# Two-layer streaming encoder on one core: an operand made a second time with the norm in it, a convolution that reads PSUM, and operand sums moved to the end of a stage

## The chip, the core and the metric

The kernel runs on one core of a Trainium2 chip. The metric is device time in microseconds (us), from the first instruction to the last. The engines in the text are PE (TensorE, matrix products), DVE (VectorE), ACT (ScalarE), POOL (GpSimd) and SP (SyncE, which here only starts transfers). ACT and POOL start transfers too, from their own instruction streams.

## The reference, cut to what matters

Two layers (`DEPTH = 2`), 512 positions, width 1024, everything in fp32:

```
h  = rmsnorm(x, norm1_g[i]);  z = h @ w_in[i] + b_in[i]
mq, mk = silu(causal_conv(z[..., :2048], conv_w[i], conv_b[i]))     # 4 taps along time
y_m = sigmoid(mo) * head_layernorm(mlstm(mq, mk, mv, mi, mf))       # 4 heads, 256 wide
y_r = silu(rg) * head_layernorm(retention(rope(rq), rope(rk), rv))  # 4 heads, 256 / 512 wide
x = x + (sigmoid(gm) * (y_m @ w_bm[i]) + sigmoid(gr) * (y_r @ w_br[i])) @ w_out[i]
x = x + relu(rmsnorm(x) @ w_ff1[i] + b_ff1[i])^2 @ w_ff2[i] + b_ff2[i]
x = x + sigmoid(rmsnorm(x) @ w_pe_gate[i]) * (p[i] @ w_pe[i])
```

The norm of a position is one number, `rstd(t)`. It can be multiplied into the operand `x * g` ahead of a product with `w_in`, or into the product's result behind it.

## The kernel before

**Products.** Activations lie transposed, as eight tiles of 128 features x 512 positions. Every fp32 operand is held as a high part (rounded to the fast fp32r form) and a low part (the rest), and a product is three matmuls (`mm3`: high x high, high x low, low x high). Weights come as a list of *units*. A `T8` unit gives one output tile 128x512 with 24 matmuls, each 512 wide. Four `V` units give the values of one head or of two (24 matmuls of 512 each). A `PAIR` unit gives two output tiles by a Strassen-Winograd scheme: seven products P1 to P7 of 12 matmuls, each 256 wide, in place of 48 matmuls that are 512 wide. It needs sums of the operand's quarters (`xs_sums`, four of them in a layer, each for two of the eight tiles of `x`) and sums of the weights' quarters, which POOL makes by software transfers, paced by the unit number. P1, P2 and P4 use the operand itself; P3, P5, P6 and P7 use its sums. P5 and P3 collect in one bank of PSUM, P1, P6 and P7 in another; after each product ACT or DVE takes out what stands there, before the next may write.

**Weights.** SP loads a unit's weights into one of four slots `wr`. ACT writes the high part `wh` (line 258), DVE the low part `wl` (line 259), two units ahead of the use.

**Order.** The code is written in the order of the stages. A scheduler of the framework then sets each engine's instruction order when the kernel is built; on the chip an engine works through its list in that order. A transfer that ACT starts is an instruction of ACT's list: if what it waits for is late, everything behind it in the list waits as well. Small working tiles come from a ring of six slots (`tmp`), PSUM has eight banks.

**A layer's first half.** `xa` is the operand `x * g` without the norm; `n1.b` is `rstd` spread over 128 rows, `n1.c` the same as columns. The stages are: the input and forget gates (`if`); the four query and key tiles of mLSTM head 0 (`l0m00` to `l0m03`, through the convolution); the values of heads 0 and 1 (`mv_vals(0)`); two tiles of the branch gate (`bgm0`, `bgm1`); then per head `m_scores`, `m_qk` of the next head (four `T8` and the convolution), `m_attend` (whose result `num` is scaled by DVE in `head_scale`, line 613), `m_out` (two output-gate tiles `o0`, `o1`, then PE transposes `num` into tiles `ot`, line 619). `xs_sums` follows `m_out(0)`, `m_out(1)`, `m_scores(2)` and `m_out(2)`, one each. Then come the retention's queries and keys (`r0brq`, `r0brk`), the product with `w_bm` (tiles `bm0` to `bm7`, each multiplied by a branch gate that is read back from `gm_spill` for the first four), and the retention heads.

**The convolution before** (`conv_evac`): DVE multiplies the PSUM tile by the norm into a padded tile `z` in SBUF (line 762), POOL fills three columns ahead of it, ACT makes the tap for the current position (line 765), DVE adds three shifted taps (line 767), ACT applies SiLU.

**Products of a PAIR before**: the norm is multiplied in behind them by `scaled` (two DVE operations 128x512 for each PAIR with `w_in`), the second with the sign that the scheme leaves.

Of the kernel before, what the change touches and what calls it, by code (L numbers as in the profile page):

```python
# [39 lines left out]
P = 128  # L41
# [15 lines left out]
PAD = 32  # L57
LAST = 4

# [42 lines left out]
def groups():  # L102

    g = {}
    for i in range(L):
# [7 lines left out]
        g[i, "gm"] = [("w_in", 0, CGM + 256 * p) for p in range(4)]  # L113
# [9 lines left out]
def unit_list(i):  # L123
# [39 lines left out]
    mo(0)  # L163
    mqk(2)
    v(CV + 512)
    mo(1)
    mqk(3)
    mo(2)
    pair("gm", 1)
    mo(3)  # L170
    rqk(0)
    for p in range(4):
        if p > 1:
            pair("gm", p)
        full("w_bm", 0, 0, 2 * p, 2 * p + 2)
    v(CRV)
# [32 lines left out]
def build(ctx, tc, ins, out):  # L209
# [50 lines left out]


    index = {g: k for k, g in enumerate(groups())}
    sums = {(g, x): tc.dram_tile([4, P, Q], F32, name=f"s{k}{x}") for g, k in index.items() for x in MADE}

    def block(g, x):
        return ins["wpairs"][index[g], GIVEN.index(x)] if x in GIVEN else sums[g, x]
# [265 lines left out]
    def rows_split_v(i, h, nm, n_, j, o, rc, bvt, vh, vl):  # L532

        t = tmp(f"{nm}v{j}")
        ve.scalar_tensor_tensor(t[:, :T], o, rc[:, j:j + 1], bvt, OP.mult, OP.add)
# [13 lines left out]
    def values(i, nm, act, nrm, bv_ap, n_):  # L549
# [3 lines left out]
        for u in range(4):  # L553
            _, wh, wl = unit("V")
            if u == 1:
                flush()
            for kk in range(2):
# [9 lines left out]
        for j in range(NT):  # L567
            rows_split_v(i, None, nm, n_, j, o[j], nrm.c, bvt, vh[j], vl[j])
# [53 lines left out]
    def gated(nm, o, nrm, func, bias):  # L622
        g = tmp(f"{nm}g")
        ve.tensor_tensor(g[:, :T], o, nrm.b, OP.mult)
        ac.activation(g[:, :T], g[:, :T], func, bias=bias)
        return g
# [92 lines left out]
    for i in range(L):  # L719
# [25 lines left out]


# [9 lines left out]
        def conv_tile(nm, c, qh, ql, q):  # L756
            conv_evac(t8(xa, f"{nm}z"), nm, c, qh, ql, q)

        def conv_evac(o, nm, c, qh, ql, q):
            z = cur["low"].tile([P, 576], F32, name=f"{nm}zp", tag="z", bufs=2)  # L760
            gp.tensor_copy(z[:, 0:3], negb[:, c:c + 1].to_broadcast([P, 3]))
            ve.tensor_tensor(z[:, 3:515], o, n1.b, OP.mult)
            a = tmp(f"{nm}cv")
            cw = [bc[:, i, ow + 16 * j + c:ow + 16 * j + c + 1] for j in range(4)]
            ac.activation(a[:, :T], z[:, 3:515], AF.Identity, bias=cbp[:, c:c + 1], scale=cw[3])
            for j in (2, 1, 0):
                ve.scalar_tensor_tensor(a[:, :T], z[:, j:j + T], cw[j], a[:, :T], OP.mult, OP.add)
# [12 lines left out]
        def m_qk(h):  # L780
            nm = f"l{i}m{h}"
            qk = qk_tiles(nm)
            for d in range(2):
                conv_tile(f"{nm}q{d}", 2 * h + d, qk[0][d], qk[1][d], True)
            for d in range(2):
                conv_tile(f"{nm}k{d}", 8 + 2 * h + d, qk[2][d], qk[3][d], False)
            return qk
# [24 lines left out]
        def m_attend(h, pt, vv):  # L812
# [3 lines left out]
            attend(nm, pt, vv[0], vv[1], (h % 2) * 258, 258, num)  # L816
            mv = head_stats(nm, num, 256)
            den = cols.tile([P, NT], F32, name=f"{nm}den", tag="den")
            dn = num[:, :, 256]
            ve.tensor_scalar(den, dn, -1.0, None, OP.mult)  # L820
            ve.tensor_tensor(den, den, dn, OP.max)
            ve.tensor_tensor(den, den, gem[:, :, h], OP.max)
            ve.reciprocal(den, den)
            hv = cols.tile([P, NT], F32, name=f"{nm}hv", tag="hv")
            ve.tensor_tensor(hv, mv[:, :, 1], den, OP.mult)
            ve.tensor_tensor(hv, hv, den, OP.mult)
            ve.tensor_scalar(hv, hv, EPS, None, OP.add)
            gp.tensor_tensor(hv, hv, nhalf, OP.pow)
            ve.tensor_tensor(hv, hv, den, OP.mult)
# [3 lines left out]
        def m_out(h, num):  # L833
            nm = f"l{i}m{h}o"
            gs = [gated(f"{nm}{v}", t8(xa, f"{nm}{v}"), n1, AF.Sigmoid, bcol(i, "bo", 2 * h + v)) for v in range(2)]
            gate_out(nm, gs, num, [bcol(i, "gmn", 2 * h + v) for v in range(2)], ym, 2 * h)

        def r_qk(h):
# [3 lines left out]
            def rope(a, bn):  # L842
                b = [bcol(i, bn, 2 * h + d) for d in range(2)]

                def consume(y):
                    for d in range(2):
                        scaled(d, y[d], n1, y[d])
                    for d in range(2):
                        u = tmp(f"{nm}{bn}u{d}")
                        w = tmp(f"{nm}{bn}w{d}")  # L850
                        ve.scalar_tensor_tensor(u, y[0], b[0], trig[d][:, :T], OP.add, OP.mult)
                        ve.scalar_tensor_tensor(w, y[1], b[1], trig[1 - d][:, :T], OP.add, OP.mult)
                        ve.tensor_tensor(u, u, w, (OP.subtract, OP.add)[d])
# [13 lines left out]
        def r_attend(h, pt, vv):  # L867
# [5 lines left out]
            ve.tensor_scalar(hv, mv[:, :, 1], EPS, None, OP.add)  # L873
# [4 lines left out]
        def r_out(h, num, y):  # L878
# [3 lines left out]
            def gates(w):  # L882
                def consume(g):
                    for d in range(2):
                        scaled(d, g[d], n1, g[d])
                        ac.activation(g[d], g[d], AF.Silu, bias=bcol(i, "brg", 4 * h + 2 * w + d))
                        gs[2 * w + d] = g[d]
# [12 lines left out]
        def gm_gates(p):  # L900

            def consume(g):
                for d in range(2):
                    scaled(d, g[d], n1, g[d])
                    gm_done(2 * p + d, g[d])
# [3 lines left out]
        def gm_done(c, g):  # L909
            ac.activation(g, g, AF.Sigmoid, bias=bcol(i, "bgm", c))  # L910
            if c < 4:
# [463 lines left out]
```

## Time and profile before

| what | value |
|---|---|
| median of three runs | 2421.15 us (2416.18 to 2422.08) |
| the profiled execution | 2422.81 us; its span 2421.1 us |
| PE busy | 2365.9 us, 98% of the span, 13860 matmuls |
| DVE busy | 1646.8 us, 68% |
| ACT busy | 1203.1 us, 50% |
| POOL busy | 257.9 us, 11% |
| mean granted PE clock | 0.989 |

The span is the time between the first and the last recorded instruction; the 1.7 us between it and the execution's time lie around it. A busy share is an average over the stages. PE's clock is the share of its full rate that the chip granted. "Waits" lists for how long an engine sat idle until a named instruction of another engine was done.

### The profile page before, as it was taken

Reading aid. Unit: us, or ns where it says so; the run is one execution under the profiler, and the core shown is the slowest. Engines: PE = TensorE matmul, PEld = TensorE weight load, DVE = VectorE, ACT = ScalarE, POOL = GpSimd, SP = SyncE. Lnnn points to the kernel's source line nnn. Section 1 sums busy time; section 2 is a strip of 40 time slices with the busy share of each in tenths; the row PEclk is TensorE's granted clock in tenths of the full one; section 3 lists DMA queues with packets and bytes.
Section 4 is the critical chain, followed back from the end, with each engine's and each line's share of the span. In section 5 each row is a group of like instructions: output and inputs, shape, how many; then the busy total and the mean of one; then the engine's idle time right before and its main releaser. Section 6 shows DMA issues by size and latency. Waiting matters only on the chain.

```text
span 2421.1 us, 35877 instructions
## 1 busy us (share of the span) xinstructions
PE 2365.9 (98%) x13860; PEld 2094.6 (87%) x13860; DVE 1646.8 (68%) x2553; ACT 1203.1 (50%) x1745; POOL 257.9 (11%) x366
## 2 busy tenths in 40 slices
PE   9898999999999999999999979999999999999997
PEld 8787888998998898899887868899989988998996
DVE  7777747775676576667777677477837756676675
ACT  5656534553454445445557554344525545455463
POOL 3211000000001200001311110000000020000011
PEclk9999999999999999999999989999999999999998
DMA  7877686667788877778766658866686885443441
GB/s 240 216 202 196 197 264 185 198 185 240 194 256 261 231 235 206 221 242 221 233 178 191 183 161 240 239 177 205 186 240 192 282 248 158 153 141 120 144 154 44
DMA packets 183371, 487.68 MB, mean 201 GB/s; under 512 B 17936, under 2 KB 20368, under 8 KB 183200
## 3 DMA queue, kind: packets, MB, share of 16 engines
q1 hardware_dynamic: 119952, 281.82, 34.9%
q0 software_dynamic: 43520, 167.78, 29.4%
q10 hardware_dynamic: 19728, 35.79, 4.2%
q8 instruction: 108, 1.77, 0.3%
q14 instruction: 63, 0.52, 0.1%
HBM read 470.64 MB, written 182.45 MB: 270 GB/s over the span
## 4 chain that ended last, share of the span: by engine, by line
PE 44%; DVE 3%; ACT 1%; issue 1%; DMA 1%; POOL 0%; POOLq 0%; DVEq 0%; ACTq 0%
PE l1f L345 2%; PE l1f L346 2%; PE l1f L347 2%; PE l1br L347 1%; PE l1br L345 1%; PE l1br L346 1%; PE l1wo L345 1%; PE l1bm L347 1%; PE l1wo L347 1%; PE l1wo L346 1%; PE l1bm L345 1%; PE l1bm L346 1%; DMA wr<-s11t 0%; DVE wl L259 0%; PE l1pg L345 0%
## 5 line engine op out<-in xcount | busy, mean ns | idle before, releaser
L258 ACT ACTIVATE wh<-wr 128x1024 fp32r<-128x1024 f32 x250 | 264.1, 1058 | 394.3 <-issue 61.8
L259 DVE TENSOR_TENSOR wl<-wr,wh 128x1024 fp32r<-128x1024 f32 x250 | 307.1, 1229 | 159.0 <-ACT wh L258 158.4
L258 ACT ACTIVATE wh_C<-wr 128x1024 fp32r<-128x1024 f32 x78 | 82.5, 1058 | 131.2 <-DMA wr<-wstream 8.8
L259 DVE TENSOR_TENSOR wl_B<-wr,wh_B 128x1024 fp32r<-128x1024 f32 x78 | 95.4, 1223 | 45.4 <-ACT wh_B L258 45.3
L258 ACT ACTIVATE wh_B<-wr 128x1024 fp32r<-128x1024 f32 x78 | 82.3, 1055 | 75.4 <-PE l0r1vp L563 3.6
L258 ACT ACTIVATE wh_A<-wr 128x1024 fp32r<-128x1024 f32 x78 | 82.4, 1057 | 71.6 <-PE l1f L346 11.3
L259 DVE TENSOR_TENSOR wl_A<-wr,wh_A 128x1024 fp32r<-128x1024 f32 x78 | 96.6, 1238 | 23.6 <-ACT wh_A L258 23.6
L258 ACT ACTIVATE wh_D<-wr 128x512 fp32r<-128x512 f32 x78 | 49.1, 629 | 123.5 <-DMA wr<-s11t 10.4
L259 DVE TENSOR_TENSOR wl_C<-wr,wh_C 128x1024 fp32r<-128x1024 f32 x78 | 95.2, 1221 | 22.1 <-ACT wh_C L258 21.3
L259 DVE TENSOR_TENSOR wl_D<-wr,wh_D 128x512 fp32r<-128x512 f32 x78 | 53.6, 688 | 80.7 <-ACT wh_D L258 73.8
L345 PE MATMUL l1f<-l1n2h,wh 128*128 128x512 f32 x256 | 99.8, 390 | 0.0
L345 PE MATMUL l0f<-l0n2h,wh 128*128 128x512 f32 x256 | 99.8, 390 | 0.0
L347 PE MATMUL l0f<-l0n2h,wl 128*128 128x512 f32 x256 | 99.7, 389 | 0.0
L347 PE MATMUL l1f<-l1n2h,wl 128*128 128x512 f32 x256 | 99.7, 389 | 0.0
L346 PE MATMUL l0f<-l0n2l,wh 128*128 128x512 f32 x256 | 99.6, 389 | 0.0
L346 PE MATMUL l1f<-l1n2l,wh 128*128 128x512 f32 x256 | 99.6, 389 | 0.0
L347 PEld LDWEIGHTS l0f<-l0n2h,wl 128*128 128x128 f32 x256 | 48.1, 188 | 10.2
L347 PEld LDWEIGHTS l1f<-l1n2h,wl 128*128 128x128 f32 x256 | 48.1, 188 | 10.2
L346 PEld LDWEIGHTS l0f<-l0n2l,wh 128*128 128x128 f32 x256 | 48.1, 188 | 9.8
L345 PEld LDWEIGHTS l1f<-l1n2h,wh 128*128 128x128 f32 x256 | 48.1, 188 | 9.8
L346 PEld LDWEIGHTS l1f<-l1n2l,wh 128*128 128x128 f32 x256 | 48.1, 188 | 9.7
L345 PEld LDWEIGHTS l0f<-l0n2h,wh 128*128 128x128 f32 x256 | 48.1, 188 | 9.6
(5788 smaller groups left out, 8368.0 us busy)
## 6 DMA issues: line engine op xcount, KB each, us to landing
wr<-wstream SPq DMA_DIRECT2D x250, 512.0 KB, 4.5
wr<-wpairs SPq DMA_DIRECT2D x234, 256.0 KB, 3.7
s0t<-wpairs POOLq DMA_DIRECT2D x6, 1024.0 KB, 9.1
s1t<-wpairs POOLq DMA_DIRECT2D x6, 1024.0 KB, 9.3
s2t<-wpairs POOLq DMA_DIRECT2D x6, 1024.0 KB, 8.8
s3t<-wpairs POOLq DMA_DIRECT2D x6, 1024.0 KB, 10.0
s4t<-wpairs POOLq DMA_DIRECT2D x6, 1024.0 KB, 9.3
s5t<-wpairs POOLq DMA_DIRECT2D x6, 1024.0 KB, 8.5
```

What stands on the lines that cost most here:

```text
L258: ac.activation(hi_ap, src, AF.Copy)
L259: ve.tensor_sub(lo_ap, src, hi_ap.bitcast(F32))
L345: te.matmul(o, sh, mh, start=first, stop=False)
L346: te.matmul(o, sh, ml, start=False, stop=False)
L347: cur["mm"] = te.matmul(o, sl, mh, start=False, stop=last)
```

## The change

1. A second operand `xn = x * g * rstd` is made in each layer, in eight steps `xn_tile(k)`: ACT starts a transfer of `x` tile k into a `tmp` slot, DVE multiplies (128x512), ACT writes the high part, DVE the low part. Tiles 0 to 3 are made beside `bgm0` and `bgm1`, tiles 4 to 7 beside the four tiles of `m_qk(1)`. Everything of the layer from the output gates of head 0 on uses it: the output gates, `m_qk(2)` and `m_qk(3)`, the second values group, `bgm2` and `bgm3`, all retention products and all PAIRs. There no norm is multiplied in behind the product: `scaled` is gone, and gates and taps read PSUM directly. `xa` is released after `m_qk(1)`, and the tiles of the operand sums take its place.
2. The convolution works on the PSUM tile: for heads 0 and 1 DVE multiplies it by the norm in place, ACT and DVE read the taps from PSUM, and a 128x3 addition (`fix`) mends the first three positions. The padded tile and POOL's copy are gone. The bank is held until the last tap.
3. The first four gate tiles are all `T8` units (before: two `T8` and a PAIR).
4. `xs_sums(0)` to `xs_sums(3)` stand together, after the values of retention head 0 and ahead of `bm0` to `bm3` and `r_qk(0)`. DVE applies gain and norm there (before: ACT the gain).
5. One unit more stands ahead of the transposes: in heads 0 and 2 the tiles `bgm2` and `bgm3`, in head 1 two units of the values, in head 3 the output gates ahead of `m_attend` and two units of the values of retention head 0 (`rv_vals(0)`, moved ahead of `bm`).
6. A few small column operations of the head norm go to POOL, and the chain of the denominator is shorter.

The built orders count 168 matmuls of 256 columns fewer and 96 of 512 more, 102 DVE instructions fewer, 16 more transfers of 256 KB on ACT.

```diff
-        g[i, "gm"] = [("w_in", 0, CGM + 256 * p) for p in range(4)]
+        g[i, "gm"] = [("w_in", 0, CGM + 256 * p) for p in (2, 3)]
...
-    def scaled(d, y, nrm, out_):
-        if d:
-            ve.scalar_tensor_tensor(out_, y, -1.0, nrm.b, OP.mult, OP.mult)
-        else:
-            ve.tensor_tensor(out_, y, nrm.b, OP.mult)
...
+        def conv_evac(o, nm, c, qh, ql, q, nrm):
             a = tmp(f"{nm}cv")
             cw = [bc[:, i, ow + 16 * j + c:ow + 16 * j + c + 1] for j in range(4)]
-            ac.activation(a[:, :T], z[:, 3:515], AF.Identity, bias=cbp[:, c:c + 1], scale=cw[3])
+            if nrm:
+                ve.tensor_tensor(o, o, nrm.b, OP.mult)
+            ac.activation(a[:, :T], o, AF.Identity, bias=cbp[:, c:c + 1], scale=cw[3])
             for j in (2, 1, 0):
-                ve.scalar_tensor_tensor(a[:, :T], z[:, j:j + T], cw[j], a[:, :T], OP.mult, OP.add)
+                t = slice(3 - j, T)
+                ve.scalar_tensor_tensor(a[:, t], o[:, :T - 3 + j], cw[j], a[:, t], OP.mult, OP.add)
+            ve.tensor_tensor(a[:, 0:3], a[:, 0:3], fix[:, :, c], OP.add)
...
+        def normed(nm, k):
+            t = tmp(f"l{i}{nm}{k}")
+            nc.scalar.dma_start(t, x_src[k])
+            ve.scalar_tensor_tensor(t, t, n1.col(k), n1.b, OP.mult, OP.mult)
+            return t
+
+        def xn_tile(k):
+            split(normed("xnr", k), xn[0][k], xn[1][k])
...
         def xs_sums(k):
-            t = [tmp(f"l{i}xsr{k}{a}") for a in range(2)]
-            for a in range(2):
-                nc.scalar.dma_start(t[a], x_src[2 * k + a])
-                ac.activation(t[a], t[a], AF.Copy, scale=n1.col(2 * k + a))
+            t = [normed("xsr", 2 * k + a) for a in range(2)]
...
         num = m_attend(0, pt, vv)
-        m_out(0, num)
-        xs_sums(0)
+        gs = m_gates(0)
+        gm_tile(2, xn, None)
+        m_back(0, gs, num)
...
         pt = m_scores(3, qk)
-        gm_gates(1)
+        gs = m_gates(3)
         num = m_attend(3, pt, vv)
-        m_out(3, num)
+        vv = rv_vals(0, lambda: m_back(3, gs, num))
...
+        for k in range(4):
+            xs_sums(k)
...
+        for c in range(4):
+            bm_tile(c)
         qk = r_qk(0)
```

**Three places of the order.** On DVE, at the start of the first layer, `cv` tiles are the convolution's sums, `ql` a low part that it leaves, and `wl_0_663` is the low weights of `bgm0`. Before:

```order
L767 SCALAR_TENSOR_TENSOR l0m00cv<-l0m00zp,bc,l0m00cv 128x512
L767 SCALAR_TENSOR_TENSOR l0m01cv<-l0m01zp,bc,l0m01cv 128x512
L762 TENSOR_TENSOR l0m02zp<-l0m0z_431,l0n1rb 128x512
L259 TENSOR_TENSOR wl_0_663<-wr_550,wh_0_662 128x1024
L762 TENSOR_TENSOR l0m03zp<-l0m0z_556,l0n1rb 128x512
L771 SCALAR_TENSOR_TENSOR l0m0ql_346<-l0m00cv,l0m0qh_345 128x512
```

After, where the low weights of `bgm0` are `wl_0_667`:

```order
L781 SCALAR_TENSOR_TENSOR l0m02cv<-l0m0z_439,bc,l0m02cv 128x511
L781 SCALAR_TENSOR_TENSOR l0m03cv<-l0m0z_561,bc,l0m03cv 128x511
L781 SCALAR_TENSOR_TENSOR l0m02cv<-l0m0z_439,bc,l0m02cv 128x510
L781 SCALAR_TENSOR_TENSOR l0m03cv<-l0m0z_561,bc,l0m03cv 128x510
L786 SCALAR_TENSOR_TENSOR l0m0ql_354<-l0m00cv,l0m0qh_353 128x512
L786 SCALAR_TENSOR_TENSOR l0m0ql_356<-l0m01cv,l0m0qh_355 128x512
L781 SCALAR_TENSOR_TENSOR l0m02cv<-l0m0z_439,bc,l0m02cv 128x509
L782 TENSOR_TENSOR l0m02cv<-l0m02cv,l0fix 128x3
L781 SCALAR_TENSOR_TENSOR l0m03cv<-l0m0z_561,bc,l0m03cv 128x509
L782 TENSOR_TENSOR l0m03cv<-l0m03cv,l0fix 128x3
L263 TENSOR_TENSOR wl_0_667<-wr_555,wh_0_666 128x1024
```

The weights of `bgm0` stood after the convolution of two tiles and now stand after that of four.

On ACT, beside attend and output gates of head 0 (after): `l0xnr_1134` is the load for the last tile of `xn`, `l0m1z_1099` the PSUM tile of head 1's last convolution, `l0m0a` the attend results.

```order
L608 ACTIVATE l0m0num<-l0m0a_1166 128x258
L608 ACTIVATE l0m0num<-l0m0a_1174 128x258
L608 ACTIVATE l0m0num<-l0m0a_1185 128x258
L262 ACTIVATE l0xnh<-l0xnr_1087 128x512
L783 ACTIVATE l0m12cv<-l0m12cv 128x512
L262 ACTIVATE wh_0_1224<-wr_999 128x1024
L262 ACTIVATE l0m1kh_948<-l0m12cv 128x512
L778 ACTIVATE l0m13cv<-l0m1z_1099,l0cbp,bc 128x512
L935 DMA l0xnr_1134<-xT 128x512
L783 ACTIVATE l0m13cv<-l0m13cv 128x512
L262 ACTIVATE l0m1kh_950<-l0m13cv 128x512
L262 ACTIVATE l0xnh<-l0xnr_1134 128x512
```

The load for the last tile stands behind the attend copies of head 0 and the last convolution of head 1; before, there was no such load.

On ACT, at the operand sums: `xsr` are the loads of `x`, `xsu` the sums, `xsh` their high parts. Before, `xs_sums(1)` stood within head 1:

```order
L936 DMA l0xsr_1832<-xT 128x512
L625 ACTIVATE l0m1o1g<-l0m1o1g,bc 128x512
L258 ACTIVATE l0ymh_333<-l0m1o0g 128x512
L936 DMA l0xsr_1833<-xT 128x512
L258 ACTIVATE l0ymh_335<-l0m1o1g 128x512
L937 ACTIVATE l0xsr_1832<-l0xsr_1832,bc 128x512
```

After, behind the values of retention head 0, the first two sets and the last:

```order
L935 DMA l0xsr_2690<-xT 128x512
L262 ACTIVATE wh_0_2793<-wr_2581 128x1024
L262 ACTIVATE l0xsh_1143<-l0xsu_2693 128x512
L935 DMA l0xsr_2703<-xT 128x512
L935 DMA l0xsr_2706<-xT 128x512
L262 ACTIVATE l0xsh_1145<-l0xsu_2694 128x512
```

```order
L262 ACTIVATE l0xsh_1155<-l0xsu_2741 128x512
L1034 DMA l0gml_2751<-gm_spill 128x512
L1034 DMA l0gml_2787<-gm_spill 128x512
L262 ACTIVATE l0xsh_1157<-l0xsu_2742 128x512
L1034 DMA l0gml_2824<-gm_spill 128x512
L1034 DMA l0gml_2860<-gm_spill 128x512
L1038 DMA bm_spill<-l0gml_2751 128x512
L1038 DMA bm_spill<-l0gml_2787 128x512
L427 ACTIVATE l0r0brqy_2904<-l0r0brqa 128x256
L1038 DMA bm_spill<-l0gml_2824 128x512
L1038 DMA bm_spill<-l0gml_2860 128x512
L429 ACTIVATE l0r0brqy_2905<-l0r0brqc 128x256
```

The loads for a set now stand behind the first sum of the set before it, and ACT's copies of the first retention PAIR (`r0brqa`, `r0brqc`) behind the gate loads and the spills of `bm0` to `bm3`.

More of the change, by code (lines that the diff above doesn't have):

```diff
@@ L163, in unit_list @@
     mo(0)
+    full("w_in", CGM, 0, 2, 3)
     mqk(2)
+    mo(1)
     v(CV + 512)
[L166 removed]
     mqk(3)
     mo(2)
[L169 removed]
+    full("w_in", CGM, 0, 3, 4)
     mo(3)
+    v(CRV)
+    full("w_bm", 0, 0, 0, 4)
     rqk(0)
[L172 to L174 removed]
+    for p in (2, 3):
+        pair("gm", p - 2)
         full("w_bm", 0, 0, 2 * p, 2 * p + 2)
[L176 removed]
     rqk(1)
@@ L556, in values @@
                 flush()
+            if u == 2 and mid:
+                mid()
             for kk in range(2):
@@ L744, in build @@
         gp.tensor_tensor(cbp, cbp, bc[:, i, oc:oc + 16], OP.add)
+        fix = cols.tile([P, 3, 16], F32, name=f"l{i}fix", tag="fix", bufs=1)
+        for j in range(3):
+            gp.tensor_tensor(fix[:, 2 - j, :], bc[:, i, ow + 16 * j:ow + 16 * j + 16], negb, OP.mult)
+            if j:
+                gp.tensor_tensor(fix[:, 2 - j, :], fix[:, 2 - j, :], fix[:, 3 - j, :], OP.add)
         _, wh, wl = unit("IF")
@@ L992, in build @@
-        qk = m_qk(3)
+        qk = m_qk(3, xn, None)
         num = m_attend(2, pt, vv)
-        m_out(2, num)
-        xs_sums(3)
+        gs = m_gates(2)
+        gm_tile(3, xn, None)
+        m_back(2, gs, num)
         pt = m_scores(3, qk)
-        gm_gates(1)
+        gs = m_gates(3)
         num = m_attend(3, pt, vv)
-        m_out(3, num)
-        trig = [cur["low"].tile([P, 576], F32, name=f"l{i}{n}", tag="z", bufs=2) for n in ("cos", "sin")]
+        vv = rv_vals(0, lambda: m_back(3, gs, num))
@@ L1017, in build @@
+        for p in (2, 3):
+            gm_gates(p)
+            bm_tile(2 * p)
+            bm_tile(2 * p + 1)
         pt = r_scores(0, qk)
```

188 lines of the change are left out of this document (93 added, 95 removed).

## The prediction

> **What bounds the kernel now.** I read the page's first part, then PE's waits, then the chain of work at the longest of them.
>
> ```profile
> span 2421.1 us, 35877 instructions
> PE 2365.9 (98%) x13860; PEld 2094.6 (87%) x13860; DVE 1646.8 (68%) x2553; ACT 1203.1 (50%) x1745; POOL 257.9 (11%) x366
> ```
>
> PE is the bound: 98% of the span, DVE 68%. So only two things can shorten the run: less PE work, or fewer and shorter waits of PE. Its waits in the part that the change touches:
>
> ```profile
> PE l1m2ot L619 <- DVE l1m2num L613: 11.4, 1, 11.4
> PE l0m2ot L619 <- DVE l0m2num L613: 7.4, 1, 7.4
> PE l0m0ot L619 <- DVE l0m0num L613: 6.4, 1, 6.4
> PE l1m0ot L619 <- DVE l1m0num L613: 3.2, 1, 3.2
> ...
> PE l1r3brkc L394 <- ACT l1r3brky L419: 0.8, 1, 0.8
> ...
> PE l1r0brkc L394 <- ACT l1r0brky L419: 0.8, 1, 0.8
> ...
> PE l0m3a L345 <- ACT l0m3ph L258: 0.7, 1, 0.7
> ...
> PE l1bgm L347 <- DVE wl L259: 0.6, 1, 0.6
> PE l0r2brkc L394 <- ACT l0r2brky L419: 0.4, 1, 0.4
> ...
> PE l0m3a L345 <- DVE l0m3p L586: 0.2, 1, 0.2
> ```
>
> Four transposes (`ot`) wait 28.4 us together, each for the scaled `num` of its head. The rows with `r2`, `r3`, `r0` and `m3a` have twins of the same size in the other layer. A wait costs more than its length, as the chain behind the longest shows (start, length, what):
>
> ```profile
> 1401.57 8.19 DMA wr<-s11t
> ...
> 1429.45 0.42 DVE l1m2num L613
> ...
> 1430.01 2.16 PE l1m2ot L619 x8
> ...
> 1433.61 0.43 PE l1m3s L346
> ...
> 1438.21 0.12 PE l1m3s L346
> ```
>
> The head waited because ACT stood at the weight sums of the gate's PAIR (8.19 us), and the convolution and the head's columns queued behind. Afterwards matmuls of 512 columns follow each other at 0.43 us. The usual distance is 0.227 (the next rows, 112.10 to 112.32), and 0.12 is that of 256 columns:
>
> ```profile
> 112.10 0.39 PE L345 MATMUL l0m0o<-l0n1h,wh 128*128 128x512 f32 x1
> 112.32 0.39 PE L346 MATMUL l0m0o<-l0n1l,wh 128*128 128x512 f32 x1
> 112.00:125.00 13.00, 6.60 (x21) 4.36 (x20) 6.18 (x12) 3.97 (x6) 1.97 (x2) 0.62 0.91 205
> ```
>
> The last row is a stretch around the first transposes: the seventh figure behind the length, 0.62, is PE's granted clock there.
>
> **The change part by part.**
>
> *A. The transposes (-40.7).* Heads 0 and 2 get 24 matmuls more of cover, 24 x 0.227 = 5.4 us, and lose work on DVE and ACT that stood ahead of the scaling (operand sums, the PAIR's weight sums, the norm of the gates). Walking the new order with the durations of the rows, `num` is scaled some 2 us ahead of need in head 0 and about 8 in head 2. So 28.4 goes. The slow stretch behind goes too: eight transposes in 2.16 us where the full rate takes half (1.1 saved), then some eight matmuls at 0.43 in place of 0.227 (1.6), 2.7 for each stall, 10.5 for four with the shorter `l1m0`. Head 3 has two gate tiles (48 x 0.227 = 10.9 us) between scores and attend, so the 0.7 + 0.2 of `m3a` goes in both layers (1.8).
>
> The Trainium skill, page "TensorE: Matmul & The Clock Gate", section "Part 1: The HAM clock gate", says that the clock is halved after an idle window of about 3.4 us and returns after about 3.4 us of sustained work. The trace agrees with 0.43 against 0.227. By that rule each long stall that the change makes would cost up to 1.7 us more behind it, an estimate from that page; two at the operand sums would add 3.4 to the sum below.
>
> *B. PE's work (+1.6).* 96 matmuls of 512 columns more and 168 of 256 fewer: 96 x 0.227 - 168 x 0.12.
>
> *C. Start of a layer (+10).* DVE's rows there:
>
> ```profile
> 53.94 0.73 DVE L767 SCALAR_TENSOR_TENSOR l0m00cv<-l0m00zp,bc,l0m00cv 128x512 f32<-128x512 f32 x1
> 54.60 0.73 DVE L767 SCALAR_TENSOR_TENSOR l0m01cv<-l0m01zp,bc,l0m01cv 128x512 f32<-128x512 f32 x1
> ...
> 57.91 0.67 DVE L762 TENSOR_TENSOR l0m02zp<-l0m0z,l0n1rb 128x512 f32<-128x512 f32 x1
> 58.51 1.20 DVE L259 TENSOR_TENSOR wl<-wr,wh 128x1024 fp32r<-128x1024 f32 x1
> ```
>
> A tap is 0.66 us from start to start, a 128x512 product with two tensors 0.60. Now two norm products (1.2) run ahead of 53.94, and ahead of `wl` stand twelve taps (7.9), two low parts (1.2) and four 128x3 additions (0.4 taken for all): `wl` starts at 64.6 and is there at 65.8.
>
> ```profile
> 61.56 0.40 PE L347 MATMUL l0bgm<-l0n1h,wl 128*128 128x512 f32 x1
> 1256.90 0.50 PE L347 MATMUL l1bgm<-l1n1h,wl 128*128 128x512 f32 x1 [0.62 <-DVE wl L259]
> ```
>
> PE wants it at 61.56: 4.2 us. In the second layer the same walk from 1250.5 gives 1261.2 against 1256.2 where PE got there: 5.0, less the 0.6 that it waits now. With 1.4 for the clock: 10. Bounds: 0, if taps from PSUM run faster and the small products are hidden, and 13. Nothing shows taps whose source is PSUM; the norm product, which reads PSUM, has the usual 0.60, so I keep 0.66.
>
> *D. Output gates of head 0 (+2.5).* The load of `xn`'s last tile is behind ACT's attend copies, a weight split and the last tap of head 1: about 8 us after PE begins that attend. Landing times on ACT's queue:
>
> ```profile
> l0xsr<-xT ACTq DMA_DIRECT2D x8, 256.0 KB, 5.2
> l1xsr<-x_spill ACTq DMA_DIRECT2D x8, 256.0 KB, 4.9
> l0gml<-gm_spill ACTq DMA_DIRECT2D x4, 256.0 KB, 4.2
> DMA to landing us min/median/max: 3.4/5.2/6.2
> DMA to landing us min/median/max: 3.6/4.9/6.3
> ```
>
> (The last two are `l0xsr` and `l1xsr`.) 8 + 5.2, DVE's product 0.66, ACT's copy 0.55, DVE's low part 0.6 and 0.6 of queue: 15.6 against 14.1 at which PE has done attend (3.6) and 46 matmuls of the tiles (10.4): 1.5 in the first layer, 1 in the second. Bounds 0 and 5.
>
> *E. The operand sums (+24).* Before, each of the four stood within a head. Now PE needs all four for P5 of the first retention PAIR. Let t0 be the end of the values ahead of them. PE then has `bm0` to `bm3`, P1, nine matmuls of P5 and six of P2: 96 x 0.227 + 27 x 0.12 = 25.0 us. Costs of a set, from before:
>
> ```profile
> L940 DVE TENSOR_TENSOR l0xsu<-l0xsr x4: 416/425/426, 124.7 to 238.1; 128x256 f32<-128x256 f32 x4
> 121.65 0.63 ACT L258 ACTIVATE l0ymh<-l0m0o0g 128x512 fp32r<-128x512 f32 x1
> 107.31 1.06 ACT L258 ACTIVATE wh<-wr 128x1024 fp32r<-128x1024 f32 x1 [1.61 <-PE l0m0o L346]
> ```
>
> ACT issues a set's loads only after the first sum of the set before is copied. One round is two issues (0.5), the landing (4.9), DVE's product and two half sums (0.66 + 2 x 0.35), ACT's copy (0.6): 7.4. The first loads leave at about t0 + 2, so the fourth sum is copied at t0 + 31, and PE waits 6 us. Then the gate loads leave; they land 4.2 later (t0 + 35.6), DVE multiplies `bm0` and `bm1`, ACT starts their spills, and only now takes out P1: t0 + 37.6. P6 may follow; P3 waits for the copy of P5 behind two more spills (39.6), P7 for that of P6 behind two weight splits of 1.06 (42.2). P7 ends at about t0 + 43.2; without waits at t0 + 96 x 0.227 + 72 x 0.12 = 30.4. That is 12.8 a layer, less the two 0.8 of `r0brkc`, whose copies now come in another order: 24. Bounds by the landing: 3.4 (and 2.7 for the gate loads) takes 7.5 off a layer, 6.3 adds 5.6. I take the medians, since these loads run among the same weight streams.
>
> *F. Retention (-2.4).* Without `scaled`, DVE and ACT are free sooner: twice 0.8 and twice 0.4 at `r3` and `r2` go. The rest of DVE's saved work (two operations for each PAIR) lies beside PE and is worth nothing; so is POOL's copy.
>
> Sum: -40.7 + 1.6 + 10 + 2.5 + 24 - 2.4 = -5. The profiled execution took 2422.81; 2417.8 on its scale, and 1.7 less against the median of 2421.15: **2416**.
>
> **The rivals.**
>
> *The sums hide (2395 to 2408, 0.23).* If the loads land at the shortest values, E falls by 15, to 2401; if C is hidden too, lower. For it: the queue's first load of a set often finds it empty. Against: medians of 4.9 and 5.2 over 16 loads, and only ACT's order matters. The Trainium skill, page "DMA: Bandwidth & Descriptors", section "Anatomy of one DMA", fits 2.0 us plus the bytes at 436 GB/s on POOL's path; for 256 KB that is 2.6 us, an estimate by which E would be 22 less and the time 2394. The rows with 4.9 speak against it.
>
> *Slower: the sums block is dearer (2429 to 2436, 0.16).* The same rounds with landings of 6.3, the longest shown, add 11 in two layers, and the slow clock behind the last wait 3: 2430. It decides from a landing of 6.2. For it: SP's 512 KB loads and POOL's sums run at that time; against: 6.3 is a single extreme.
>
> *The change doesn't do what it says (about 2430, 0.07).* The transposes still wait, because in the new order the scaling stands on DVE behind the product of the last `xn` tile. From a landing some 2 us longer than the median the cover in head 0 is used up; with half of A's waits given back, 14 more. Against: in head 2 no such load is ahead.
>
> **How the numbers follow.** About 0.3%, 7.3 us, is what a measurement of this kernel tells from no change: faster is below 2413.9, slower above 2428.4. The forecast, 2406 to 2426 around 2416, has 0.54: of it 0.19 below 2413.9 and 0.35 within. The first rival adds 0.23 to faster; of the last two, 0.22 are slower and 0.01 within. Range: from 2395, where the shortest landings and half of C's bound meet, to 2433.
>
> **What would show it.** No wait of `ot` above 1 us (A). PE waits of some 4 to 5 us at `bgm` for `wl` in each layer (C). One to two us at `m0o` for `xnl` or `xnh` (D). At `r0brqc` PE waits some 6 us for `xsh` or `xsl`, and again at `r0brqa` for ACT (E); loads of `xsr` in four pairs, 7 to 8 us apart. No waits at `r2brkc` and `r3brkc` (F). I am wrong if the four pairs lie closer, if `bgm` doesn't wait, or if a stage that I hold for covered (head 1 with its transposes within the values, or PSUM banks held by the convolution) shows a wait.

## The result and the profile after

The changed kernel is slower: 2446.39 us (median of five runs) against 2422.08 in the same comparison, a ratio of 1.0098 with a 95% interval from 1.0074 to 1.0123. I forecast 2416 with a range to 2433. The profiled execution has a span of 2445.7 us against 2421.1.

The top of the profile page of the kernel after, and then PE's waits in it:

```profile
span 2445.7 us, 35635 instructions
PE 2378.4 (97%) x13788; PEld 2097.4 (86%) x13788; DVE 1589.8 (65%) x2451; ACT 1188.6 (49%) x1730; POOL 251.7 (10%) x368
```

```profile
PE l1r0brqc L404 <- ACT l1xsh L262: 7.8, 2, 5.5
PE l0r0brqa L404 <- ACT l0r0brqy L427: 4.4, 1, 4.4
PE l0bgm L357 <- DVE wl L263: 4.1, 1, 4.1
PE l1n41ss L508 <- ACT l1n41sq L491: 3.9, 1, 3.9
PE l1bgm L357 <- DVE wl L263: 3.9, 1, 3.9
PE l0r0brqc L404 <- ACT l0xsh L262: 3.2, 1, 3.2
PE l1r0brqa L404 <- ACT l1r0brqy L427: 2.8, 1, 2.8
PE l1m0o L356 <- DVE l1xnl L263: 2.5, 2, 1.6
PE l1f L355 <- ACT l1n2h L477: 2.5, 1, 2.5
...
PE l0m0o L355 <- ACT l0xnh L262: 1.8, 1, 1.8
...
PE l0f L355 <- ACT l0n2h L477: 1.6, 1, 1.6
...
PE l0m0o L356 <- DVE l0xnl L263: 1.5, 1, 1.5
PE l1m0o L357 <- DVE wl L263: 1.5, 1, 1.5
```

No `ot` is left in it: the transposes wait for nothing. In their place stand `bgm`, `m0o` and `r0brq`, which were forecast, and the first feed-forward tiles (`f`), which were not. (`n41ss` waited 4.0 us before the change too.)

Where the time went, from the start of the first matmul of one tile to that of another, in us. "No waits" is the shortest time that the same matmuls took in any run (for heads 0 and 2, which issue the same ones, in either head). In the rows of these two heads the kernel after has 24 matmuls more.

| stretch | before, layers 1 / 2 | after | no waits (before / after) |
|---|---|---|---|
| `gtp` to `m0rp` (two gate tiles) | 12.06 / 13.30 | 19.05 / 19.04 | 12.06 |
| `m0o` to `m1s` (gates, transposes of head 0) | 20.39 / 15.42 | 24.48 / 25.05 | 12.30 / 17.74 |
| `m1s` to `m2s` | 64.79 / 65.14 | 63.40 / 63.39 | 63.34 / 63.38 |
| `m2o` to `m3s` (the same in head 2) | 21.29 / 25.24 | 17.74 / 17.75 | 12.30 / 17.74 |
| `m3s` to `r1brqa` (head 3, sums, `bm`, `r0`) | 144.62 / 144.40 | 141.86 / 151.12 | - |
| `r1brqa` to `wo` | 383.97 / 383.97 | 381.73 / 381.73 | - |
| `f` to `o00a` (first ff tiles) | 55.85 / 55.89 | 61.73 / 62.57 | 55.85 |

Two chains of the trace show what the late stretches have in common. The first, of the changed kernel, is the sums block of the second layer, and behind it stand POOL's transfers of that time (start, length, what; of a transfer in the first list the length runs to its landing, in the second it is the issue alone):

```profile
1490.78 8.64 DMA l1xsr<-x_spill
1499.45 0.77 DVE l1xsr L936
...
1501.18 9.31 DMA l1xsr<-x_spill
1510.52 0.75 DVE l1xsr L936
...
1512.42 7.30 DMA l1xsr<-x_spill
```

```profile
1489.27 0.91 POOL L300 DMA_DIRECT2D s14t<-wpairs  x1 [10.84 <-PE l1r0vp L573]
1500.13 0.90 POOL L300 DMA_DIRECT2D s15t<-wpairs  x1 [9.95 <-PE l1bm L357]
1510.96 0.58 POOL L300 DMA_DIRECT2D s15t<-s15t  x1 [9.94 <-PE l1bm L357]
```

It is the round that I walked, set by set, but with landings (from a load's issue to its arrival) of 8.64, 9.31 and 7.30 us in place of 4.9. Each load left 1.1 to 1.5 us behind a weight sum of 1 MB. The first two sums took 9.96 and 10.16 us to land, and each load behind them landed within 0.3 us of its sum. The second chain is the end of the product with `w_out` in the first layer:

```profile
809.05 8.81 DMA l0xr<-xT
...
819.77 0.67 DVE l0n2l L478
...
820.49 0.50 PE l0f L356
```

```profile
808.09 0.92 POOL L300 DMA_DIRECT2D s8t<-wpairs  x1 [1.87 <-PE l0wo L357]
```

The last load of `x` for the second norm left 1.0 us behind a weight sum and landed after 8.81 us, 0.3 us ahead of that sum; before the change it took 4.6. And at head 0's gates, DVE's own list (start, length; the bracket is idle time ahead and what ended it):

```profile
106.28 0.74 DVE L781 SCALAR_TENSOR_TENSOR l0m11cv<-l0m1z,bc,l0m11cv 128x511 f32<-128x511 f32 x1
106.94 0.74 DVE L781 SCALAR_TENSOR_TENSOR l0m10cv<-l0m1z,bc,l0m10cv 128x509 f32<-128x509 f32 x1
107.59 0.15 DVE L782 TENSOR_TENSOR l0m10cv<-l0m10cv,l0fix 128x3 f32<-128x3 f32 x1
108.79 0.75 DVE L936 SCALAR_TENSOR_TENSOR l0xnr<-l0xnr,bc,l0n1rb 128x512 f32<-128x512 f32 x1 [1.04 <-DMA l0xnr<-xT]
109.45 0.74 DVE L781 SCALAR_TENSOR_TENSOR l0m11cv<-l0m1z,bc,l0m11cv 128x510 f32<-128x510 f32 x1
112.11 0.75 DVE L936 SCALAR_TENSOR_TENSOR l0xnr<-l0xnr,bc,l0n1rb 128x512 f32<-128x512 f32 x1 [1.92 <-DMA l0xnr<-xT]
```

DVE stood 1.04 and 1.92 us at two loads for tiles of `xn`, with the taps of head 1 behind them in its list. The second of these loads took 7.47 us, from 104.62.

### The profile page after: what moved, and what is told of

It is laid out like the page before. It is cut to its first block, busy times and chain, and to the rows that moved or that the text cites. A ratio compares the mean times of both kernels' runs of the same rounds, so it can differ in the third digit from the quotient of the medians.

```text
span 2445.7 us, 35635 instructions
## 1 busy us (share of the span) xinstructions
PE 2378.4 (97%) x13788; PEld 2097.4 (86%) x13788; DVE 1589.8 (65%) x2451; ACT 1188.6 (49%) x1730; POOL 251.7 (10%) x368
## 3 DMA queue, kind: packets, MB, share of 16 engines
q8 instruction: 108, 1.77, 0.3%
## 4 chain that ended last, share of the span: by engine, by line
PE 85%; DVE 5%; DMA 5%; issue 3%; ACT 1%; POOL 0%; ACTq 0%; POOLq 0%; DVEq 0%
PE l1f L356 2%; PE l1f L355 2%; PE l1f L357 2%; PE l0f L356 2%; PE l0f L357 2%; PE l0f L355 2%; PE l1br L357 1%; PE l0br L357 1%; PE l0br L355 1%; PE l1br L355 1%; PE l0br L356 1%; PE l1br L356 1%; DMA l1xsr<-x_spill 1%; DMA l1xr<-x_spill 1%; DMA l0xnr<-xT 1%
## 5 line engine op out<-in xcount | busy, mean ns | idle before, releaser
L355 PEld LDWEIGHTS l1f<-l1n2h,wh 128*128 128x128 f32 x256 | 48.6, 190 | 12.7 <-ACT l1n2h L477 2.9
L357 PEld LDWEIGHTS l0f<-l0n2h,wl 128*128 128x128 f32 x256 | 48.6, 190 | 10.3
L357 PEld LDWEIGHTS l1f<-l1n2h,wl 128*128 128x128 f32 x256 | 48.6, 190 | 10.3
```

What stands on the lines that cost most here:

```text
L355: te.matmul(o, sh, mh, start=first, stop=False)
L357: cur["mm"] = te.matmul(o, sl, mh, start=False, stop=last)
```

## The experiments

My theory: the waits at `bgm`, `m0o`, `r0brq` and `f` are the loss, each with its own cause in the order, and three of the four are made long by loads that run beside POOL's weight sums. The rivals were that DVE is simply full at the start of a layer, and that the transposes' waits come back as soon as anything is moved. The kernel before was run alongside each time: its median was 2421.58 us with runs 1 to 4, 2426.39 with runs 5 to 8 and 2421.09 with runs 9 to 11. So runs of different groups, and the changed kernel with its 1.0098, are compared by their ratios to it. Stretches and waits come from one profiled execution of each run.

**1. The pace of the weight sums set back.**

```diff
-    return 3 + 5 * min(k, 20) // 4 + 7 * max(k - 20, 0) // 4
+    n = 3 + 5 * min(k, 20) // 4 + 7 * max(k - 20, 0) // 4
+    return n + (n >= 36) + (n >= 200)
```

> The pace of POOL's weight sums is set back by as many units as the change put into the list (one from the 36th unit on, one more from the 200th), nothing else. Theory: in the changed kernel the first ff tiles wait because the last load of x for the second norm runs beside a 1 MB weight sum that falls one unit earlier against it; the ff start then loses its 5.9 and 6.7 us in the two layers: span about 2433 against 2446, ff stages as before the change. Rival: the load is late because ACT issues it late (order, slots), whatever runs beside it: span stays within 2443 to 2448 and ff's first tiles still wait.

Measured: 2438.92 us, ratio 1.0067 (1.0043 to 1.0090). The first ff start is 55.85 us again, the second 62.76. Half of the theory at most: this pace doesn't put both layers right, and the first start is 55.85 in runs 2, 3, 6 and 8 as well, where the pace is untouched. `m3s` to `r1brqa` rose by 4.1 and 1.9 us to 145.93 and 152.98, and the profiled span is 2441.6.

**2. The operand sums back in the heads.**

```diff
         m_back(0, gs, num)
+        xs_sums(0)
...
+        xs_sums(1)
         pt = m_scores(2, qk)
+        xs_sums(2)
...
         m_back(2, gs, num)
+        xs_sums(3)
...
-        for k in range(4):
-            xs_sums(k)
```

> The four operand sums go back to where they stood before the change (behind the output of heads 0 and 2, behind the second values, behind the scores of head 2); everything else of the change stays. Theory: the waits at r0brqc and r0brqa go, which with their slow clock cost 11 us in the first and 20 us in the second layer, and the heads have the cover for it: span 2414 to 2420, no transposes wait over 1 us. Rival: the sums bring the heads' waits back, since the transposes wait whenever ACT and DVE carry the sums: r0 loses its waits, but the ot tiles wait 10 us or more in all and the span is 2430 or above.

Measured: 2416.09 us, ratio 0.9969 (0.9954 to 0.9983), 0.3% below the kernel before. `m3s` to `r1brqa` falls to 131.53 and 135.82, and no transposes wait. What is left at the head of PE's waits:

```profile
PE l0bgm L357 <- DVE wl L263: 4.1, 1, 4.1
PE l1n41ss L508 <- ACT l1n41sq L491: 3.9, 1, 3.9
PE l1bgm L357 <- DVE wl L263: 3.9, 1, 3.9
PE l1m3a L355 <- ACT l1m3ph L262: 2.4, 1, 2.4
```

The rival falls: the transposes of the heads carry the sums without waiting. The last row is new: in the second layer PE waits 2.4 us for ACT at the attend of head 3. Net of that, gathering the sums at the stage's end cost 10.3 and 15.3 us. The ff starts were 55.85 and 56.56 here with the pace untouched. In the first layer they hang on tenths of a microsecond: the last load of `x` left 0.35 to 0.58 us behind the same weight sum in runs 2, 3, 6 and 8, and all four take 55.85; it left 0.95 us behind it in the changed kernel and 1.88 in run 4, which take 61.73 and 62.18. In the second layer such a rule doesn't come out: 0.57 to 0.60 us in runs 2, 3, 4, 6 and 8 went with starts of 56.56 to 65.74.

**3. The loads of `xn` ahead of the convolution beside them.**

```diff
+                if between:
+                    between(d)
                 conv_evac(o, f"{nm}{d}", 8 * (d // 2) + 2 * h + d % 2, qk[2 * (d // 2)][d % 2],
                           qk[2 * (d // 2) + 1][d % 2], d < 2, nrm)
-                if between:
-                    between(d)
```

> In head 1 each load and making of a tile of the second operand is written ahead of the convolution of the tile beside it, so that the last load leaves ahead of head 0's attend copies; nothing else. Theory: the output gates of head 0 no longer wait for the last tile (6.8 and 7.3 us in the two layers): span 2431 to 2435. Rival: the convolution of head 1 or head 0's scaling now comes later by the same work, and the wait moves to the transposes or to the scores of head 1: span 2442 or above.

Measured: 2449.09 us, ratio 1.0108 (1.0083 to 1.0133): the rival. `m0o` to `m1s` falls by 2.3 and 2.9 us, but in the second layer a new wait stands ahead of `m0o`:

```profile
PE l1m0o L355 <- DVE l1m10cv L782: 6.3, 1, 6.3
```

PE wants the PSUM bank that the first convolution tile of head 1 still holds, because DVE now waits for loads ahead of its taps: 6.24 us at the load for a tile of `xn`, between the first and the second tap of that convolution tile. That is the price of a convolution that works in PSUM.

**4. The convolution of head 0's last two tiles behind the first gate tile.**

```diff
+                held.clear()
...
-            if d < 2:
-                held.append((o, a))
-            else:
-                conv_evac(o, *a)
+            held.append((o, a))
...
             gm_tile(c, xa, n1)
+            for o_, a in held:
+                conv_evac(o_, *a)
+            held = []
```

> At the start of a layer the convolution of the third and fourth tile of head 0 is written behind the first branch gate tile, so that the low weights of that tile stand ahead of it on DVE, as before the change; nothing else. Theory: bgm no longer waits for wl; the layer starts lose 7.0 and 5.7 us: span 2432 to 2435. Rival: DVE is the bound of that stretch, and the scores of head 0 wait in place of bgm for the late convolution: span 2442 or above, with a wait at m0s.

Measured: 2438.51 us, ratio 1.0069 (1.0047 to 1.0090), between the two forecasts. `gtp` to `m0rp` is 12.06 in both layers, as without waits, but the scores now wait:

```profile
PE l0m0s L355 <- ACT l0m0kh L262: 5.4, 1, 5.4
...
PE l1m0s L355 <- ACT l1m0kh L262: 3.7, 1, 3.7
```

This stretch and the one behind it, `m0rp` to `m0o`, are together 49.2 and 47.2 against 48.8 and 48.8: the wait moved. Here the convolution stood behind the taking out of the values, too late; run 6 puts it between.

**5. The changed kernel without weight sums.**

```diff
-        dma = gp.dma_start(flat(block(g, x)), flat(block(g, MADE[x][a])), max_dma_last_dim=4096, **kw)
-        tc.add_manual_dep(dma.ins, cur["mm"].ins.name, SYNC, reason="pace of the sums")
...
-                    nc.sync.dma_start(r[:, k * Q:(k + 1) * Q], block(g, y)[p])
+                    nc.sync.dma_start(r[:, k * Q:(k + 1) * Q], block(g, {'t1': 'B12', 't2': 'B22', 't3': 'B12', 't4': 'B21'}.get(y, y))[p])
```

> The changed kernel without POOL's weight sums: no such transfer is issued, and the PAIRs read given weight blocks in their place, so the products of the PAIRs are other numbers, with the same instructions and sizes on the other engines. Theory: loads of 256 KB on ACT's queue land in 7 to 10 us where they are issued beside or just behind a 1 MB weight sum, and that is what makes the second layer's sums block dearer than the first's, the output gates of head 0 wait in both layers and the ff starts wait. Without the sums the medians of xsr, xnr and xr landings fall to 2.5 to 4 us, ff starts lose their 12.6 us, m0o most of its 14 us, the two r0 stages come out alike and cost at most 8 us each; span 2405 to 2415. Rival: the serial order on ACT and DVE alone makes these stalls; landings hardly move and the span stays above 2430.

Measured: 2404.28 us, ratio 0.9912 (0.9884 to 0.9941), just below the theory's range. The span is 2401.3 against 2445.7. The median landings of the loads of `x` on ACT's queue without sums, and then the least, the median and the most of `l1xsr` in the changed kernel:

```profile
l1xnr<-x_spill ACTq DMA_DIRECT2D x8, 256.0 KB, 2.7
l1xsr<-x_spill ACTq DMA_DIRECT2D x8, 256.0 KB, 2.9
...
l1xr<-x_spill ACTq DMA_DIRECT2D x8, 256.0 KB, 2.6
```

```profile
DMA to landing us min/median/max: 2.7/5.1/9.3
```

(The second fence goes by the five of the eight loads whose landing the trace gives; the 8.64 and the 7.30 shown above are not among them.)

`m0o` and `f` are gone from PE's waits, both ff starts take 55.85, `m0o` to `m1s` falls to 19.10 and 17.88, and the two layers' sums blocks come out alike (137.24 and 137.30). What stays is `bgm` with 4.1 and 3.9 and `r0brqa` with 3.2 in each layer: these two belong to the order alone, and so does a new 1.3 at `bgm2c` in each layer. The Trainium skill, page "DMA: Bandwidth & Descriptors", section "Anatomy of one DMA", gives by its fit for POOL's path 2.6 us for 256 KB, an estimate; without the sums the medians of 2.6 to 2.9 agree, beside them 5.1 with a most of 9.3 does not.

**6. Sums spread, and the convolution between two units of the values** (on top of run 2).

```diff
+                held.clear()
...
-            if d < 2:
-                held.append((o, a))
-            else:
-                conv_evac(o, *a)
-        vv = mv_vals(0, xa, n1.c)
+            held.append((o, a))
+        vv = mv_vals(0, xa, n1.c, lambda: [conv_evac(o_, *a) for o_, a in held])
```

> The version with the operand sums spread over the heads as before the change, and at a layer's start the convolution of head 0's third and fourth tile written between the second and third unit of the values, behind the preparation of the first branch gate's weights and ahead of the taking out of the values. Theory: bgm loses its 4 us wait for wl and its slow clock (12 us in two layers at most) without a wait of the scores in its place, as DVE's list now stands as before the change: median 2404 to 2409. Rival: DVE has no room there at all, the wait moves to the scores (as it did when the convolution stood behind the gate tile): 2413 to 2418.

Measured: 2401.86 us, ratio 0.9897 (0.9873 to 0.9921). `gtp` to `m0rp` is 12.18 and 12.06 and the scores don't wait. So it was the place of `wl` in DVE's list, and DVE has the room.

**7. As 6, head 0's gates on the first operand and `xn` made later.**

```diff
-            xn_tile(2 * c)
-            xn_tile(2 * c + 1)
+            xn_tile(c)
...
-        qk = m_qk(1, xa, n1, lambda d: xn_tile(4 + d))
+        qk = m_qk(1, xa, n1, lambda d: xn_tile(2 + d))
+        num = m_attend(0, pt, vv)
+        gs = [gated(f"l{i}m0o{v}", t8(xa, f"l{i}m0o{v}"), n1, AF.Sigmoid, bcol(i, "bo", v)) for v in range(2)]
+        xn_tile(6)
+        gm_tile(2, xa, n1)
+        xn_tile(7)
...
-        num = m_attend(0, pt, vv)
-        gs = m_gates(0)
-        gm_tile(2, xn, None)
```

> As the version before, and the two output gates of head 0 and the third branch gate tile use the first operand with the norm behind the product, as before the change; the tiles of the second operand are made later (one beside each of the two first gate tiles, four beside head 1, two beside the gates of head 0). Theory: the wait for xnh and xnl at m0o and its slow clock go (7 us a layer), as nothing needs the second operand before head 2: median 2390 to 2400. Rival: DVE has the same work in the same stretch, so head 0's transposes or head 2's first tiles wait instead: 2405 or above.

Measured: 2407.26 us, ratio 0.9923 (0.9900 to 0.9946): the rival. `m0o` to `m1s` stays at 26.64 and 26.35; only the name of the wait changed:

```profile
PE l0bgm L357 <- DVE wl L263: 6.6, 1, 6.6
PE l1bgm L357 <- DVE wl L263: 5.8, 1, 5.8
```

That `bgm` is now the third gate tile. In the first layer DVE stands 4.40 us at the load for a tile of `xn`, in the second 1.84, and works almost without a gap from there to the `wl` that PE wants: what stands in DVE's list behind the making of `xn` is late here too.

**8. As 2, without the extra unit ahead of the transposes.**

```diff
-        gm_tile(2, xn, None)
         m_back(0, gs, num)
         xs_sums(0)
+        gm_tile(2, xn, None)
```

(The same in head 2 with the fourth gate tile.)

> The version with the sums spread, but with the third and fourth branch gate tiles behind the transposes of heads 0 and 2, so that only the two output gates cover the scaling there; nothing else. Theory: the extra unit of 5.4 us is what covers the scaling in head 0, which has some 2 us to spare with it: the transposes of head 0 wait 3 to 5 us in each layer with slow clock behind, head 2 less: median 2422 to 2432. Rival: the waits were made by the gate's PAIR and its weight sums alone, which are gone here: median 2413 to 2419, no transposes wait over 1 us.

Measured: 2421.90 us, ratio 0.9985 (0.9973 to 0.9996), just below the 2422 that I gave. Its ratio is 0.0016 above that of run 2, some 4 us, with intervals that overlap. The waits are back, smaller than before the change:

```profile
PE l1m0ot L628 <- DVE l1m0num L622: 3.3, 1, 3.3
...
PE l1m2ot L628 <- DVE l1m2num L622: 1.7, 1, 1.7
PE l0m0ot L628 <- DVE l0m0num L622: 1.6, 1, 1.6
```

The fourth, `l0m2ot`, waits 0.3. In the two profiles the rows of heads 0 and 2 are together 13.1 us longer than in run 2, and `m3s` to `r1brqa` is 5.4 shorter in both layers together.

**9. The kernel before without weight sums** (the same edit as in 5).

> The kernel before the change, without POOL's weight sums (the PAIRs read given weight blocks, so their products are other numbers). Theory: the changed kernel suffers more from these transfers, because its chains of loads (second operand, sums block, second norm) have no slack; without them the kernel before gains only what its transposes lose to the late weight sums of the gate's PAIR (about 8 us of the 11.4) and a few us more: span 2400 to 2412, so that the change without the sums is worth 0 to 10 us of gain instead of a loss of 24. Rival: the weight sums cost both kernels the same, some 44 us, and the kernel before falls to about 2378.

Measured: 2397.25 us, ratio 0.9906 (0.9878 to 0.9933); span 2393.7. Its transposes wait only in head 2:

```profile
PE l0m2ot L616 <- DVE l0m2num L610: 4.3, 1, 4.3
PE l1m2ot L616 <- DVE l1m2num L610: 4.3, 1, 4.3
```

Both theories were off: by the profiled spans the sums cost the kernel before 27 us and the changed one 44; by the ratios it is 23 and 45. So of the loss of 24 to 25 us, 17 (by the ratios 22) come with the sums, and 7.6 stay without them (2401.3 against 2393.7). By the ratios, 0.9912 and 0.9906, only 1.5 stay, with intervals that overlap, so that this rest isn't clear of noise. The run also says that two thirds of the waits that the change was to remove (28.4 against 8.6), and those of head 0 wholly, came with these transfers.

**10. The loads for the second norm two tiles earlier** (in the changed kernel).

```diff
+        xrs = []
...
-            xr = tmp(f"l{i}xr{c}")
-            nc.scalar.dma_start(xr[:, :T], x_src[c])
+            while len(xrs) < min(KT, c + 3):
+                xrs.append(tmp(f"l{i}xr{len(xrs)}"))
+                nc.scalar.dma_start(xrs[-1], x_src[len(xrs) - 1])
+            xr = xrs[c]
```

> The changed kernel, in which the loads of x for the second norm are issued two tiles earlier (the same loads, on the same queue); nothing else. Theory: the ff start waits since a load that is issued only one tile ahead lands 8 to 9 us later where a 1 MB weight sum runs; with two tiles more ahead the wait goes in both layers: the ff starts are 55.9 again, 12.6 us together, median about 2434. Rival: the chain waits for something else, or the earlier loads only crowd the queue: 2443 to 2448.

Measured: 2441.65 us, ratio 1.0089 (1.0055 to 1.0124). Both ff starts take 55.85: 12.6 us less there, as expected. The ratio is only 0.0009 below that of the changed kernel, some 2 us, with intervals that overlap. In the profile the span is 7.1 us shorter (2438.6): the first layer's `m3s` to `r1brqa` was 145.17, 3.3 above that of the changed kernel, and PE waited 7.4 us there for `xsh` at `r0brqc` in place of 3.2.

**11. Sums spread, convolution between the units, loads earlier** (6 and 10).

> The version with the sums spread and the convolution between the units of the values, and with the loads for the second norm two tiles earlier. Theory: its second layer's ff start loses the 5.7 us that it still waited: median 2395 to 2398. Rival: the ff start of that version was a chance of one profile, and nothing moves: 2400 to 2404.

Measured: 2398.85 us, ratio 0.9913 (0.9888 to 0.9939), between the two forecasts. It is the lowest median of the kernels with weight sums, but the ratio of run 6 is lower still and the intervals overlap, so that the time doesn't tell the two apart. Both ff starts take 55.85, as the theory had it, and what is left at the head of PE's waits that the change made is the making of `xn`:

```profile
PE l0m0o L355 <- ACT l0xnh L262: 3.5, 2, 3.1
PE l1m0o L355 <- ACT l1xnh L262: 3.5, 2, 3.1
```

Some 15 us lie there still: `m0o` to `m1s` is 26.0 and 24.4 against 17.74 without waits.

## Why the prediction was wrong

The sum was -5 us; the span grew by 24.6. The step that failed is the price of a load. Every load on ACT's queue was walked with the median landing of its name, 4.2 to 5.2 us, and with 6.3 as the longest. That put D at 2.5 us where 14.0 were measured, and left the first ff tiles out, where 12.6 were. By the terms, from the table:

- **A, the transposes: right in size, half right in its reason.** Head 0 lost 20.39 - 12.30 = 8.1 and 3.1 us of waits with their slow clock, head 2 9.0 and 12.9, `m1s` to `m2s` 1.4 and 1.8: 36.3, and the rest in head 3 within a stretch where other things moved. 40.7 was said. The extra unit is the smaller part of it: run 8, without that unit, finds 6.9 us of waits at the transposes where there were 28.4, and 13.1 us more in the rows of the two heads than run 2. The larger part came with the other edits of those heads (the gate's PAIR and its weight sums gone, shorter lists on DVE), which no run took apart.
- **C, start of a layer: right in kind, small.** 7.0 + 5.7 = 12.7 against 10; waits of 4.1 and 3.9 against 4.2 and 5.0. The other 5.3 us (12.7 less the two waits, of which 0.6 stood there before) lie at and behind them, where the granted clock was 0.56 and 0.58 (66 to 70 and 70 to 74 us in the first layer); 1.4 was said for that. The walk of the second layer has a slip: 1261.2 is where `wl` starts, it would be there at 1262.4, and the wait by that walk is 6.2. Run 6 shows the cause, `wl` behind twelve taps.
- **D, output gates of head 0: where it failed first.** 2.5 was said; the stretches grew by 24.48 - 17.74 = 6.7 and 7.3: 14. I walked only the load of the last tile of `xn`. In the first layer PE stopped at the fifth and at the seventh of the eight tiles, and not at the eighth. On DVE the products of the tiles before the last stand ahead of head 1's taps and of the low parts and wait for their loads (1.04 and 1.92 us of idle in the rows above, the second at a load of 7.47 us). The bound of 5 that I gave was for a late last load, not for a list that stops at each. Nor had D a term for the slow clock, which is some 2.8 of the 6.7. Without the weight sums (run 5) these stretches are 19.10 and 17.88, so the late landings made most of it.
- **E, the operand sums: right in kind.** The rounds, the gate loads behind them and ACT's late copies are there as walked. Run 2 gives 10.3 and 15.3, 25.6 together against 24. That the sum fits is partly luck: the layers differ by the landing, which was 3.3 in the median in the first and 5.1 in the second, up to 9.3, and one came out below the 12 of a layer and one above. The four pairs of loads left 6 to 8.5 us apart in the first layer and 9 to 12 in the second, where 7 to 8 was said. Without the weight sums and with landings of 2.9 the block still takes 137.3, against 131 in run 8, which has the sums in the heads: some 6 us a layer belong to the order, more than the 4.5 that the working left with landings of 3.4.
- **F, retention: 4.5 less** against 2.4.
- **Left out: the first ff tiles, 5.9 + 6.7 = 12.6.** The working has no term behind the retention, where no instruction changes. The last load of `x` left about a microsecond behind a weight sum there and landed late. Run 5 shows it (without the sums both starts are 55.85), and run 10 (with the loads issued earlier, 55.85 too). Why it met the sum is not shown: the list of units is one longer in each layer and the sums are paced by unit number, but runs 2, 3, 6 and 8 have that same pace and don't wait in the first layer.

The common fault of D, E and the ff start is the landing time. I took medians of 4.2 to 5.2 for loads of which each waits for the one before. In the kernel before, the landings of `x` that the trace gives lie between 2.8 and 6.3, so these rows didn't show the 7 to 9 us of the changed kernel. Other rows of it did: two spills of 256 KB from ACT's queue (`bm_spill`) took 9.36 and 9.16 us, 0.6 and 2.0 us behind a weight sum of 1 MB. A chain of loads takes whichever landing it meets, and a chain without slack hands each late one to PE. The rival "the sums block is dearer" had the right side, 2430, and got 0.16; alone it would not have reached 2446, and its landing, 6.3 as the longest, was too short as well.

One reading of the working is off without any weight in the sum: the granted clock of 0.62 is the sixth figure behind the length, not the seventh.

The first matmul of `m0z` in the first layer came 2.4 us later in the profile of the changed kernel than in that before (`if` to `m0z`: 8.31 against 5.95). In the other runs of this study that stretch lay between 5.70 and 8.88 without an order to it; what sets it stays open.

## What to carry to other kernels

Price a load by what runs beside it when it is issued, not by the median of its name, and look for lists in which work that is ready stands behind an instruction that waits for a load. Loads that each wait for the last belong spread over stages that have cover, or issued several steps ahead; put together, they are a chain as long as their sum. And look beyond the stages that a change touches: a load that leaves some tenths of a microsecond later behind a large transfer can cost a wait there.

## What the runs showed of the hardware

- Loads of `x` of 256 KB landed in medians of 2.6 to 3.1 us where no weight sums of POOL ran (runs 5 and 9), and in the changed kernel in up to 9.31 us when they left about a microsecond behind a sum of 1 MB. Two that left only 0.07 and 0.52 us behind one (309.34 and 309.79 in the first layer) landed in 2.62 and 3.32. All weight sums together cost the kernel before 27 us of span by the profiles, 23 by the ratios.
- PE's clock fell without a long gap. Ahead of the slow stretch PE waited 1.52 and 1.77 us, with five matmuls between. The next two matmuls of 512 columns came 0.72 and 0.60 us apart, and ten more 0.43 us apart; from 119 to 122 us the granted clock was 0.50:

```profile
115.51 0.50 PE L356 MATMUL l0m0o<-l0xnl,wh 128*128 128x512 f32 x1 [1.52 <-DVE l0xnl L263]
...
118.70 0.80 PE L355 MATMUL l0m0o<-l0xnh,wh 128*128 128x512 f32 x1 [1.77 <-ACT l0xnh L262]
119.42 0.80 PE L356 MATMUL l0m0o<-l0xnl,wh 128*128 128x512 f32 x1
120.02 0.63 PE L357 MATMUL l0m0o<-l0xnh,wl 128*128 128x512 f32 x1
120.44 0.63 PE L355 MATMUL l0m0o<-l0xnh,wh 128*128 128x512 f32 x1
```

  Against 0.227 us from start to start that is some 2.8 of D's 6.7 us in the first layer, an estimate from these distances. The Trainium skill, page "TensorE: Matmul & The Clock Gate", section "Part 1: The HAM clock gate", speaks of an idle window of about 3.4 us; here two shorter waits within 4.7 us were enough.
- Taps that read PSUM took what taps from SBUF took: 0.74 us each against 0.73 before the change, and 0.66 from start to start in both (the rows of DVE above and in the prediction). The 128x3 addition took 0.15.
